# Feed-forward up projection of a decoder trunk: the second block of each loaded pair by seven half-size products in place of eight

## The chip, the cores and the metric

One core of one Trainium2 chip. The metric is the time of one execution on the device in microseconds (us), from which a median is taken over several runs. Times inside the profile are of one profiled execution of the same kernel.

## The reference, cut to what matters

```python
def _swiglu(h, w_up, w_down):
    u, gte = _split(h @ w_up, [D_FF, D_FF])
    return (jax.nn.silu(u) * gte) @ w_down
...
# each of DEPTH = 2 layers, every sub-layer wrapped as
#   x <- LN(alpha * x + gate * sublayer(modulate(x)))
#   feed-forward, token mixer (three branches and an out projection), feed-forward
```

The sizes are D_MODEL = 1024, SEQ = 512 tokens, D_FF = 2816, all float32. There are four feed-forwards (called FFN0 to FFN3 here, two per layer). Each computes 2816 columns of u and 2816 columns of g from 1024 inputs for 512 tokens, multiplies silu(u) by g, and projects back to 1024.

## The kernel before, in words

**Products.** A float32 product is made of three matmuls. Every operand is split into `hi` (rounded to the matmul's type) and `lo` (what is left), and `mm3` (L199 to L203) adds hi by hi, one cross term and the other cross term into the same PSUM bank. The activations stand in SBUF as `hhi` and `hlo`, 8 blocks of 128 inputs by 512 tokens. Weights come by DMA (SP's queue) into a ring of three `raw` tiles of 2048 floats and are split by `split_w` (L186): ACT copies `hi` (L194), and DVE subtracts `lo` (L196), or POOL where `on_pool` is set. That is so for chunk 0 of FFN1 to FFN3 and in the mixers.

**Slots.** The split weights live in slots that rotate (`slot`, L156): four in the pool `weights` ("base") and five more in a pool that is opened per stage ("ext", `WEXT`). A mode, base, ext or all, says which of them the next split takes. A split has to wait until the matmuls that read the slot's last content are done.

**One feed-forward** (`ffn`, L452). The 2816 columns are 22 blocks of 128, and they are worked in five chunks of 4, 4, 4, 5 and 5 blocks. In a chunk, each block is two products, u and g, of 8 input blocks by three matmuls of 512 tokens (24 and 24 matmuls of 128x512). Each has its own PSUM bank, from a rotation of four. Then ACT takes silu (L479), DVE multiplies (L480), and the result is split into `ahi` and `alo` (ACT L649, DVE L650). After the chunk's blocks, its down projection adds 128x512 products into eight banks, those of the rotation among them (`token_major`, `accumulators`). Chunks 0 to 3 are then evicted to the residual by DVE (`evict`, L553 and L554); the last chunk runs the norms of the next stage (`finish`, L410, `modulate`). In chunks 1 to 4 the blocks are loaded in pairs, one raw tile of u and one of g for two blocks. Chunk 0 is made while the previous stage's norms end: its first three blocks run in halves of 256 tokens, and block 3 as a whole. Between the blocks `bg_step` runs pieces of a vector by matrix product on DVE (L282, L284) for later stages.

**Order.** A scheduler writes each engine's list ahead of time. At run time every engine works through its list in order and waits by semaphores.

The changed code touches `ffn` (the chunk's loop over pairs), `ada` in its form for the start of the program, the mixer's out projection, and the size of the ext pool.

Of the kernel before, what the change touches and what calls it, by code (L numbers as in the profile page):

```python
# [9 lines left out]
F32 = mybir.dt.float32  # L10
# [21 lines left out]
WBASE = {"raw": 3, "hi": 4}  # L32
WEXT = {"raw": 0, "hi": 5}
BANKS = {"g": 2, "s": 3, "r": 2, "c": 1}
# [25 lines left out]
class Trunk:  # L60
    def __init__(self, ctx, tc, a, out):
# [3 lines left out]
        self.n = 0  # L65
        self.on_pool = False
        self.wmode, self.wcount = "all", {"raw": -1, "hi": -1}
# [182 lines left out]
    def ada(self, l, v, q, dst, mul=1.0):  # L250
# [6 lines left out]
        if self.starting:  # L257

            ps = self.ps("c")
            for kk in range(0, KB, 4):  # L260
                rs = [self.we.tile([P, 2, 512], F32, tag=tag, bufs=WEXT["hi"], name=self.nm("ada")) for tag in ("hi", "lo")]
                for i, r in enumerate(rs):
# [171 lines left out]


    def token_major(self, acc, lhs, rhs, first, last, kbs, by_tile, then=None, halves=False):

# [20 lines left out]
    def ffn(self, l, f, sub, nxt, begin):  # L458
# [3 lines left out]
        with self.tc.tile_pool(name=self.nm("ffn"), bufs=1, reuse_waits="tile") as fp:  # L462
# [10 lines left out]
            def up_mm(pss, ws, *part):  # L473
                for ps, w in zip(pss, ws):
                    self.gemm_part(ps, w, *part)

            def up_act(pss, hi, lo):
# [10 lines left out]
            for c, n in enumerate(CHUNKS):  # L488
# [26 lines left out]
                while j < n:  # L515
                    m = min(2, n - j)
                    for i, r in enumerate(up_load(b0 + j, m)):
                        pss = [self.ps("g"), self.ps("g")]
                        with later(c):
                            ws = [self.split_w(w) for w in r]  # L520
                        up_mm(pss, ws, 0, S)
                        up_act(pss, ahi[:, j + i, :], alo[:, j + i, :])
# [802 lines left out]
    def mixer(self, l, nxt):  # L1325
# [175 lines left out]
```

## Time and profile before

| | |
|---|---|
| median of 3 runs | 3094.02 us (3092.88 to 3103.51) |
| the profiled execution | 3098.59 us |
| its span (first to last instruction) | 3096.5 us |
| mean granted TensorE clock | 0.983 |
| PE busy | 2931.2 us, 95% of the span |
| DVE busy | 1880.0 us, 61% |
| ACT busy | 1142.2 us, 37% |
| POOL busy | 554.8 us, 18% |

The four feed-forwards lie at about 0 to 370 us, 1183 to 1555, 1555 to 1925 and 2725 to 3096; the mixers lie between. PE is TensorE's matmuls, PEld its loading of weights. A timeline row gives the start, the duration, the engine, the line, the operation, the output and inputs, and in brackets the idle time before it with what ended it. A matmul's duration runs from its start to its modelled end and overlaps the next one's, so the pace is read from start to start.

### The profile page before, as it was taken

To read this page: it belongs to the slowest core of one execution; us is meant where nothing else is said; L and a number is where in the kernel's file an instruction comes from. 1 tells how busy PE (TensorE), PEld (TensorE's weight loads), DVE (VectorE), ACT (ScalarE), POOL (GpSimd) and SP (SyncE) were. 2 spreads that over 40 slices of the span, in tenths; PEclk is the share of its full clock that TensorE was granted. 3 is DMA by queue.
4 is the path that set the end of the run, shared out by engine and by line. 5 is a ranking of instruction groups with operands and counts; after the bars stand their busy time and mean duration, and the time that the engine had idled before them with its cause. 6 is when DMAs were issued, how large, how long until landed. Compare 5 with 4: busy or idle time off the path is not lost. (4 is left out here: it accounts for less than half of the span.)

```text
span 3096.5 us, 39351 instructions
## 1 busy us (share of the span) xinstructions
PE 2931.2 (95%) x15330; PEld 2338.4 (76%) x15330; DVE 1880.0 (61%) x3534; ACT 1142.2 (37%) x1699; POOL 554.8 (18%) x379
## 2 busy tenths in 40 slices
PE   7999998998989998999999999889989899999998
PEld 5888886676766788888888887767666677788887
DVE  6755567666785656565656546667676756654435
ACT  4322253332545635222342214433335554342212
POOL 0000142333232013000130002423333320230000
PEclk9999999999999999999999999999999999999999
DMA  8634333333342463434434424433333424632221
GB/s 280 224 109 146 115 117 101 88 87 102 94 113 67 139 203 118 139 122 143 129 117 136 133 92 145 127 99 93 88 90 93 107 73 143 204 116 96 89 68 62
DMA packets 389402, 372.17 MB, mean 120 GB/s; under 512 B 54964, under 2 KB 318544, under 8 KB 389216
## 3 DMA queue, kind: packets, MB, share of 16 engines
q1 hardware_dynamic: 377048, 350.14, 37.0%
q10 hardware_dynamic: 12168, 19.53, 1.7%
q8 instruction: 120, 1.97, 0.3%
q14 instruction: 66, 0.54, 0.1%
HBM read 347.54 MB, written 22.09 MB: 119 GB/s over the span
## 5 line engine op out<-in xcount | busy, mean ns | idle before, releaser
L194 ACT ACTIVATE hi<-raw 128x1024 fp32r<-128x1024 f32 (+1 forms) x460 | 469.2, 1028 | 1248.9 <-PE pg L202 501.3
L196 POOL TENSOR_TENSOR lo<-raw,hi 128x1024 fp32r<-128x1024 f32 x164 | 408.0, 2490 | 1692.1 <-ACT hi L194 1639.2
L201 PE MATMUL pg<-hhi,hi 128*128 128x512 f32 (+1 forms) x1744 | 680.4, 393 | 13.7 <-DVE ks L645 3.7
L202 PE MATMUL pg<-hlo,hi 128*128 128x512 f32 (+1 forms) x1744 | 673.5, 389 | 2.9 <-DVE nm L343 2.9
L203 PE MATMUL pg<-hhi,lo 128*128 128x512 f32 (+1 forms) x1744 | 674.8, 391 | 0.0
L196 DVE TENSOR_TENSOR lo<-raw,hi 128x1024 fp32r<-128x1024 f32 (+1 forms) x296 | 342.5, 1165 | 301.3 <-ACT hi L194 296.1
L201 PEld LDWEIGHTS pg<-hhi,hi 128*128 128x128 f32 x1744 | 330.9, 190 | 86.9 <-issue 10.5
L203 PEld LDWEIGHTS pg<-hhi,lo 128*128 128x128 f32 x1744 | 330.6, 190 | 66.5 <-issue 2.1
L202 PEld LDWEIGHTS pg<-hlo,hi 128*128 128x128 f32 x1744 | 331.2, 190 | 65.3 <-issue 4.7
L202 PE MATMUL pr<-hlo,hi 128*128 128x512 f32 (+1 forms) x816 | 300.4, 368 | 5.1 <-DVE nm L343 2.9
L201 PE MATMUL pr<-hhi,hi 128*128 128x512 f32 (+1 forms) x816 | 301.5, 370 | 2.2 <-ACT hhi L397 2.2
L203 PE MATMUL pr<-hhi,lo 128*128 128x512 f32 (+1 forms) x816 | 300.7, 369 | 0.0
L284 DVE SCALAR_TENSOR_TENSOR acc<-raw,cact,acc 128x512 f32<-128x512 f32 x224 | 187.7, 838 | 48.7 <-DMA raw<-in_ada_w_dram 44.3
L202 PEld LDWEIGHTS pr<-hlo,hi 128*128 128x128 f32 x816 | 155.0, 190 | 34.2 <-issue 7.4
L201 PEld LDWEIGHTS pr<-hhi,hi 128*128 128x128 f32 x816 | 155.1, 190 | 28.1 <-ACT hhi L397 2.6
L203 PEld LDWEIGHTS pr<-hhi,lo 128*128 128x128 f32 x816 | 155.2, 190 | 27.4
L352 POOL TENSOR_TENSOR rstd<-var,mhalf 128x1 f32<-128x1 f32 x48 | 30.2, 630 | 470.5 <-DVE var L351 461.9
L201 PE MATMUL ps<-hi,ahi 128*128 128x512 f32 x264 | 103.5, 392 | 0.0
L203 PE MATMUL ps<-hi,alo 128*128 128x512 f32 x264 | 103.3, 391 | 0.0
L202 PE MATMUL ps<-lo,ahi 128*128 128x512 f32 x264 | 103.1, 391 | 0.0
L480 DVE TENSOR_TENSOR su<-pg,su 128x512 f32<-128x512 f32 x42 | 28.9, 689 | 115.2 <-PE pg L203 115.1
L480 DVE TENSOR_TENSOR su<-pr,su 128x512 f32<-128x512 f32 x42 | 29.0, 690 | 110.0 <-PE pr L203 105.9
(443 smaller groups left out, 4956.9 us busy)
## 6 DMA issues: line engine op xcount, KB each, us to landing
raw<-in_ffn_up_dram SPq DMA_DIRECT2D x70, 1024.0 KB
raw<-in_w_in_dram SPq DMA_DIRECT2D x132, 512.0 KB
raw<-in_ada_w_dram SPq DMA_DIRECT2D x64, 1024.0 KB
raw<-in_ffn_down_dram SPq DMA_DIRECT2D x40, 1024.0 KB
raw<-in_ffn_up_dram SPq DMA_DIRECT2D x36, 512.0 KB
gspill<-gate ACTq DMA_DIRECT2D x48, 256.0 KB
gate<-gspill SPq DMA_DIRECT2D x48, 256.0 KB
ada<-in_ada_w_dram SPq DMA_DIRECT2D x16, 512.0 KB
```

The lines of the kernel that those rows point to most:

```text
L194: self.nc.scalar.activation(hi, v, AF.Copy)
L196: eng.tensor_tensor(out=lo, in0=v, in1=hi.bitcast(F32), op=ALU.subtract)
L201: mm(out=ps, lhsT=lhi, rhs=rhi, start=start, stop=False, **kw)
L202: mm(out=ps, lhsT=lhi, rhs=rlo, start=False, stop=False, **kw)
L203: return mm(out=ps, lhsT=llo, rhs=rhi, start=False, stop=stop, **kw).ins
L284: nc.vector.scalar_tensor_tensor(out=acc, in0=r[:, i, :], scalar=c, in1=acc, op0=ALU.mult, op1=ALU.add)
L352: nc.gpsimd.tensor_tensor(out=r, in0=v, in1=self.mhalf, op=ALU.pow)
L480: nc.vector.tensor_tensor(out=su, in0=pss[1], in1=su, op=ALU.mult)
```

## The change

In chunks 1 to 4 the second block of every pair is no longer computed by two products of 8 input blocks by 512 tokens. The pair (u, g) of that block is seen as a 2 by 2 arrangement of weights (u and g, by input blocks 0 to 3 and 4 to 7), and the activations as 2 by 2 (input blocks 0 to 3 and 4 to 7, by tokens 0 to 255 and 256 to 511). Eight products of a quarter each would make that; the changed code makes it of seven (Strassen's scheme in Winograd's form). So 84 matmuls of 128x256 stand for 48 of 128x512. It is done for 8 blocks of each feed-forward, 32 in all.

- `combine` makes four sums of activation quarters once per feed-forward, in front of chunk 0's down projection: four operations of 128x1024 on DVE, four on POOL, then four splits (ACT L460, DVE L461) into eight new `T` tiles. It borrows `lng`, `lnb` and `gb` as scratch, so the load of `gb` for the feed-forward (L317) comes after it.
- `weight_sums` makes four sums of weight quarters per pair, all on POOL (128x512 each, L471 to L474). `seven_weights` splits u's weights, the two tiles of sums and half of g's. That last half has one buffer of its own (`g2hi`, `g2lo`).
- `seven` runs the seven products into three banks x, y and z. Running sums are carried in the banks, with copies by ACT between products (L503, L507, L509, L511), adds by DVE (L505, L514) and POOL (L512), one silu (L515), and two multiplications (L517, L518).
- To make room for T, the ext pool has 2 slots instead of 5. The program's first loads, the mixer's out projection and the last chunk's down projection take their slots accordingly.

```diff
-WEXT = {"raw": 0, "hi": 5}
+WEXT = {"raw": 0, "hi": 2}
...
+    def combine(self):
+        a, b, d = (t.rearrange("p (k s) -> p k s", k=4) for t in (self.lng, self.lnb, self.gb))
...
+        v(out=a, in0=hi[1], in1=lo[1], op=ALU.add)
+        g(out=b, in0=hi[3], in1=lo[3], op=ALU.add)
+        v(out=c, in0=a, in1=hi[0], op=ALU.subtract)
+        v(out=c, in0=c, in1=lo[0], op=ALU.subtract)
+        g(out=d, in0=b, in1=a, op=ALU.subtract)
+        v(out=a, in0=b, in1=c, op=ALU.subtract)
+        g(out=b, in0=hi[2], in1=a, op=ALU.subtract)
+        g(out=b, in0=b, in1=lo[2], op=ALU.add)
+        for i, t in enumerate((a, c, d, b)):
+            nc.scalar.activation(self.T[i][0], t, AF.Copy)
+            v(out=self.T[i][1], in0=t, in1=self.T[i][0].bitcast(F32), op=ALU.subtract)
...
+    def seven_weights(self, u, g, a, b):
+        for v in (u, a, b):
+            hi, lo = self.split_w(v)
+            ws += [(hi[:, k], lo[:, k]) for k in (k1, k2)]
+        hi, lo = (self.we.tile([P, 4, P], F32R, tag=n, name=self.nm(n)) for n in ("g2hi", "g2lo"))
+        self.split_act(g[:, k2], hi, lo)
+        return ws + [(hi, lo)]
...
+        product(0, x, True)
+        act(s1, x, AF.Copy)
+        product(1, y, True)
+        v(out=s1, in0=s1, in1=y, op=ALU.add)
+        product(2, x, False)
+        act(s2, x, AF.Copy)
+        product(3, z, True)
+        act(p5, z, AF.Copy)
+        product(4, x, False)
+        act(u3, x, AF.Copy)
+        nc.gpsimd.tensor_tensor(out=u3, in0=u3, in1=p5, op=ALU.add)
+        product(5, z, False)
+        v(out=s2, in0=s2, in1=z, op=ALU.add)
+        act(su, su, AF.Silu)
+        product(6, x, False)
+        v(out=s1, in0=s1, in1=x, op=ALU.mult)
+        v(out=s2, in0=s2, in1=u3, op=ALU.mult)
...
+                    rs = up_load(b0 + j, m)
+                    if c and m == 2:
+                        sums = self.weight_sums(*rs[1])
+                    for i, r in enumerate(rs):
+                        if c and i:
+                            up_pair(r, sums, ahi[:, j + i, :], alo[:, j + i, :])
...
                 if c == 0:
+                    self.combine()
...
-                ws += [self.split_w(r[:, i : i + 1, :], *((xp, 1) if k + i == KB - 1 else ())) for i in range(2)]
+                if k == 6:
+                    self.wmode = "base"
...
+                ws += [self.split_w(r[:, i : i + 1, :], *((xp, 2) if k == 4 else ())) for i in range(2)]
```

Three places of the order are shown. In the changed program L194 and L196 are still `split_w`, L747 is `split_act`, L570 the silu of an ordinary block.

ACT's list during a block of seven products, in chunk 1 of FFN0 (`su_1119` is that block's sum, `hc` holds P5 and U3, `s` are the sums of weights):

```order
L194 ACTIVATE hi_1303<-raw_1226 128x1024
L747 ACTIVATE ahi_1018<-su_1088 128x512
L503 ACTIVATE su_1119<-pg_1120 128x256
L194 ACTIVATE hi_1307<-s_1230 128x1024
L507 ACTIVATE su_1119<-pg_1120 128x256
L194 ACTIVATE hi_1311<-s_1231 128x1024
L509 ACTIVATE hc_1123<-pr_1122 128x256
L511 ACTIVATE hc_1123<-pg_1120 128x256
L194 ACTIVATE hi_1439<-raw_1437 128x1024
L515 ACTIVATE su_1119<-su_1119 128x512
L747 ACTIVATE g2hi_1315<-raw_1228 128x512
L747 ACTIVATE ahi_1018<-su_1119 128x512
```

Three splits for a later block now stand among the copies out of PSUM, one in front of the copies L507 and L509 each. All 32 blocks have this order.

POOL's list at the start of FFN1, before (raw_10124 and raw_10114 are chunk 0's down weights, raw_10039 holds block 3's u and g):

```order
L196 TENSOR_TENSOR lo_10127<-raw_10124,hi_10126 128x1024
L196 TENSOR_TENSOR lo_10131<-raw_10124,hi_10130 128x1024
L196 TENSOR_TENSOR lo_10045<-raw_10039,hi_10044 128x1024
L196 TENSOR_TENSOR lo_10049<-raw_10039,hi_10048 128x1024
L196 TENSOR_TENSOR lo_10117<-raw_10114,hi_10116 128x1024
L196 TENSOR_TENSOR lo_10121<-raw_10114,hi_10120 128x1024
```

and now (block 3's weights are raw_10544, u first and g second; the down weights are raw_10644 and raw_10654):

```order
L452 TENSOR_TENSOR lnb_9746<-hhi,hlo 128x1024
L455 TENSOR_TENSOR gb_9744<-lnb_9746,lng_9745 128x1024
L457 TENSOR_TENSOR lnb_9746<-hhi,lng_9745 128x1024
L458 TENSOR_TENSOR lnb_9746<-lnb_9746,hlo 128x1024
L196 TENSOR_TENSOR lo_10550<-raw_10544,hi_10549 128x1024
L196 TENSOR_TENSOR lo_10651<-raw_10644,hi_10650 128x1024
L196 TENSOR_TENSOR lo_10657<-raw_10654,hi_10656 128x1024
L196 TENSOR_TENSOR lo_10661<-raw_10654,hi_10660 128x1024
L196 TENSOR_TENSOR lo_10554<-raw_10544,hi_10553 128x1024
L196 TENSOR_TENSOR lo_10647<-raw_10644,hi_10646 128x1024
L471 TENSOR_TENSOR s_10786<-raw_10784 128x512
```

The four operations of `combine` stand ahead of all of them, and the `lo` of block 3's g has moved from fourth of six to ninth of ten, behind three of the down weights.

ACT's list a little later in the same stage, now (`su_10605` is block 3, raw_10782 and raw_10784 are the first pair of chunk 1):

```order
L570 ACTIVATE su_10539<-pc_10327 128x512
L194 ACTIVATE hi_10646<-raw_10644 128x1024
L747 ACTIVATE ahi_10202<-su_10539 128x512
L747 ACTIVATE g2hi_10877<-raw_10784 128x512
L194 ACTIVATE hi_10794<-raw_10782 128x1024
L570 ACTIVATE su_10605<-pg_10547 128x512
```

The half split of g for chunk 1's first pair stands in front of block 3's silu. Its raw tile is loaded by SP behind the reload of `gb`, and takes the place in the ring of a down tile of which POOL's `lo_10647` is the last reader. Before, the four splits of the first pair (u and g of both its blocks) stood ahead of block 3's silu.

## Rows read from the trace of the kernel before

**Rows 1.** The page, part 1: busy time and share of each engine.

```profile
PE 2931.2 (95%) x15330; PEld 2338.4 (76%) x15330; DVE 1880.0 (61%) x3534; ACT 1142.2 (37%) x1699; POOL 554.8 (18%) x379
```

**Rows 2.** Waits of PE, 1206 to 1550 us (FFN1): us in total, times, longest.

```profile
PE pg L201 <- DVE su L480: 0.6, 1, 0.6
PE pc L374 <- ACT xn L368: 0.4, 1, 0.4
```

**Rows 3.** The same, 1540 to 1620 us (from FFN1 into FFN2).

```profile
PE pr L202 <- DVE var L351: 2.2, 1, 2.2
PE pr L201 <- ACT hhi L397: 2.2, 1, 2.2
```

**Rows 4.** Timeline of PE: four blocks, from their first matmul to the down projection's first.

```profile
1256.48 0.39 PE L201 MATMUL pr<-hhi,hi 128*128 128x512 f32 x1
...
1301.28 0.39 PE L201 MATMUL pr<-hi,ahi 128*128 128x512 f32 x1
```

**Rows 5.** Timeline of PE: matmuls of 128x256, two stretches of chunk 0 of FFN1.

```profile
1193.42 0.28 PE L201 MATMUL pr<-hhi,hi 128*128 128x256 f32 x1
...
1197.66 0.28 PE L201 MATMUL pr<-hhi,hi 128*128 128x256 f32 x1
...
1206.28 0.28 PE L201 MATMUL pg<-hhi,hi 128*128 128x256 f32 x1
...
1210.02 0.28 PE L201 MATMUL pg<-hhi,hi 128*128 128x256 f32 x1
```

**Rows 6.** Groups by line and shape, weight loads: busy us, mean ns, idle before.

```profile
L202 PEld LDWEIGHTS pg<-hlo,hi 128*128 128x128 f32 x1744 | 331.2, 190 | 65.3 <-issue 4.7
```

**Rows 7.** Groups by line and shape, ACT.

```profile
L194 ACT ACTIVATE hi<-raw 128x1024 fp32r<-128x1024 f32 x428 | 449.2, 1058 | 1195.9 <-PE pg L202 475.8 <-PE pr L202 325.7 <-PE ps L203 156.8
L649 ACT ACTIVATE whi<-wf 128x256 fp32r<-128x256 f32 x16 | 6.4, 401 | 0.0
```

**Rows 8.** Groups by line and shape, DVE and POOL.

```profile
L196 DVE TENSOR_TENSOR lo<-raw,hi 128x1024 fp32r<-128x1024 f32 x264 | 320.5, 1223 | 300.1 <-ACT hi L194 294.9
...
L196 DVE TENSOR_TENSOR lo<-raw,hi 128x512 fp32r<-128x512 f32 x32 | 21.9, 686 | 1.2 <-ACT hi L194 1.2
...
L196 POOL TENSOR_TENSOR lo<-raw,hi 128x1024 fp32r<-128x1024 f32 x164 | 408.0, 2490 | 1692.1 <-ACT hi L194 1639.2 <-PE pg L203 16.9 <-DMA wf<-in_rwkv_w_dram 12.9
...
L1275 POOL TENSOR_TENSOR bout<-i,ge 128x512 f32<-128x512 f32 x16 | 21.8, 1365 | 137.6 <-DVE i L1274 123.5 <-ACT Y L894 14.1
```

**Rows 9.** Timelines of POOL and DVE at the start of FFN1.

```profile
1181.88 2.62 POOL L196 TENSOR_TENSOR lo<-raw,hi 128x1024 fp32r<-128x1024 f32 x1 [0.95 <-ACT hi L194]
...
1215.38 8.12 POOL L196 TENSOR_TENSOR lo<-raw,hi 128x1024 fp32r<-128x1024 f32 x3 [2.75 <-ACT hi L194]
...
1182.18 3.40 DVE L399 TENSOR_TENSOR hlo<-hf,hhi 128x1024 fp32r<-128x1024 f32 x1
...
1216.91 1.52 DVE L650 TENSOR_TENSOR alo<-su,ahi 128x512 fp32r<-128x512 f32 x1 [0.70 <-ACT ahi L649]
```

**Rows 10.** Windows of FFN1 (stretch; busy us of PE, PEld, DVE, ACT, POOL; PEclk; DMA).

```profile
1206.00:1234.50 28.50, 28.50 (x200) 26.37 (x200) 14.54 (x17) 13.16 (x16) 12.63 (x5) 1.00 0.52 165
...
1256.40:1301.20 44.80, 44.80 (x194) 36.18 (x193) 23.18 (x29) 12.23 (x15) 0.00 (x0) 1.00 0.48 153
1301.20:1323.00 21.80, 21.80 (x98) 18.02 (x97) 13.00 (x19) 4.85 (x5) 0.00 (x0) 1.00 0.20 72
```

**Rows 11.** Windows at the start of FFN2, the same columns.

```profile
1561.00:1564.00 3.00, 0.62 (x3) 0.41 (x3) 3.00 (x4) 1.33 (x3) 1.84 (x1) 0.89 0.04 3
1564.00:1567.00 3.00, 2.93 (x14) 2.96 (x15) 2.46 (x8) 1.32 (x2) 0.86 (x1) 0.50 0.88 328
```

**Rows 12.** Timelines of SP, ACT, DVE and PE, chunk 0 of FFN1.

```profile
1208.16 10.12 SPq L182 DMA_DIRECT2D raw<-in_ffn_up_dram  x2
...
1213.29 2.01 ACT L194 ACTIVATE hi<-raw 128x1024 fp32r<-128x1024 f32 x2 [1.24 <-DMA raw<-in_ffn_up_dram]
...
1202.28 1.22 DVE L399 TENSOR_TENSOR hlo<-hf,hhi 128x1024 fp32r<-128x1024 f32 x1 [1.19 <-ACT hhi L397]
...
1222.60 0.39 PE L201 MATMUL pg<-hhi,hi 128*128 128x512 f32 x1
...
1233.59 0.39 PE L201 MATMUL pr<-hi,ahi 128*128 128x512 f32 x1
```

More of the change, by code (lines that the diff above doesn't have):

```diff
@@ L65, in __init__ @@
         self.n = 0
-        self.on_pool = False
+        self.on_pool, self.etile = False, -1
         self.wmode, self.wcount = "all", {"raw": -1, "hi": -1}
@@ L260, in ada @@
             for kk in range(0, KB, 4):
-                rs = [self.we.tile([P, 2, 512], F32, tag=tag, bufs=WEXT["hi"], name=self.nm("ada")) for tag in ("hi", "lo")]
+                rs = []
+                for _ in range(2):
+                    i = self.etile = (self.etile + 1) % 12
+                    tag, bufs = (("T", 8), ("hi", WEXT["hi"]), ("T", 8), ("T", 8), ("lo", WEXT["hi"]), ("T", 8))[i % 6]
+                    rs.append(self.we.tile([P, 2, 512], F32, tag=tag, bufs=bufs, name=self.nm("ada")))
                 for i, r in enumerate(rs):
@@ new lines, in weight_sums @@
+    def weight_sums(self, u, g):
+        nc = self.nc
+        a, b = (self.lp.tile([P, D], F32, tag="xn", bufs=2, name=self.nm("s")).rearrange("p (k c) -> p k c", k=KB) for _ in range(2))
+        t = nc.gpsimd.tensor_tensor
+        k1, k2 = slice(0, 4), slice(4, 8)
+        t(out=a[:, k2], in0=g[:, k1], in1=g[:, k2], op=ALU.add)
+        t(out=a[:, k1], in0=a[:, k2], in1=u[:, k1], op=ALU.subtract)
+        t(out=b[:, k1], in0=u[:, k1], in1=g[:, k1], op=ALU.subtract)
+        t(out=b[:, k2], in0=u[:, k2], in1=a[:, k1], op=ALU.subtract)
+        return a, b
@@ new lines, in seven_weights, with seven, product @@
+    def seven_weights(self, u, g, a, b):
+        k1, k2 = slice(0, 4), slice(4, 8)
+        ws = []
+        for v in (u, a, b):
[4 more added lines that the diff above has]
+        return ws + [(hi, lo)]
+    def seven(self, ws, su):
+        nc = self.nc
+        act, v = nc.scalar.activation, nc.vector.tensor_tensor
+        x, y, z = (self.ps("g")[:, 0:256] for _ in range(3))
+        c = self.lp.tile([P, KB, P], F32, tag="hf", bufs=1, name=self.nm("hc")).rearrange("p k s -> p (k s)")
+        p5, u3 = c[:, 0:256], c[:, 256:512]
+        s1, s2 = su[:, 0:256], su[:, 256:S]
+        def product(i, out, start):
+            (whi, wlo), (rhi, rlo) = ws[i], self.h7[i]
+            for k in range(4):
+                self.mm3(out, whi[:, k, :], wlo[:, k, :], rhi[:, k, :], rlo[:, k, :], start and k == 0, k == 3, skip_group_check=True)
+        product(0, x, True)
[15 more added lines that the diff above has]
+        v(out=s2, in0=s2, in1=u3, op=ALU.mult)
@@ L475, in up_mm, with up_pair @@
                     self.gemm_part(ps, w, *part)
+            def up_pair(r, sums, hi, lo):
+                ws = self.seven_weights(*r, *sums)
+                su = fp.tile([P, S], F32, tag="su", bufs=2, name=self.nm("su"))
+                self.seven(ws, su)
+                self.split_act(su, hi, lo)
             def up_act(pss, hi, lo):
@@ L516, in ffn @@
                     m = min(2, n - j)
[L517 to L522, printed above, removed]
+                    rs = up_load(b0 + j, m)
[4 more added lines that the diff above has]
+                            up_pair(r, sums, ahi[:, j + i, :], alo[:, j + i, :])
+                        else:
+                            pss = [self.ps("g"), self.ps("g")]
+                            with later(c):
+                                ws = [self.split_w(w) for w in r]
+                            up_mm(pss, ws, 0, S)
+                            up_act(pss, ahi[:, j + i, :], alo[:, j + i, :])
                         if c:
```

8 lines of the change are left out of this document (added).

## The prediction, made before the changed kernel was run

> **What bounds the kernel now.** I read the page's totals first, to see which engine there is to save on: PE is busy for 95% of the span, DVE for 61%, POOL for 18% [rows 1]. Whether a cut in PE's work is a cut in time then depends on whether PE waits, so the second view is PE's waits in a feed-forward. From 1206 to 1550 us, chunks 0 to 4 of FFN1, it waited 1.0 us in all [rows 2]. The reader is to see there that the feed-forward is bound by the issue of matmuls alone. Only where one stage passes into the next does PE stand, for example 2.2 and 2.2 us into FFN2, on the norm's chain of DVE and ACT operations [rows 3]. So every microsecond of matmul taken out counts in full, unless a wait appears that has no row yet. The third view, the timelines, is where I looked for such waits: what an engine would need to be late by.
>
> **What it removes.** Four ordinary blocks, 192 matmuls of 128x512, run from 1256.48 to 1301.28, 44.80 us, 0.2333 us each [rows 4]. A block is 48 of them, 11.20 us. It becomes 84 of 128x256. Their pace has two rows: 36 in 4.24 us (0.1178) and 33 in 3.74 us (0.1133) [rows 5]. I take half of the 512's own pace, 0.1167, because both shapes stand at the same granted clock of 1.00 [rows 10] and it lies between the two. Then the seven cost 9.80 us and a block gains 1.40; 32 blocks gain **44.8 us**. With 0.1133 it would be 53.8, with 0.1178 41.7: the bounds. A weight load shows 190 ns of busy time [rows 6], more than a 256's pace, but the 256s of rows 5 each came with their own load, so loads overlap and I give them no price.
>
> The trace's steps of 0.2333 and 0.1133 to 0.1178 can be set against a rule. The Trainium skill, "TensorE: Matmul & The Clock Gate", section "Back-to-back issue gap", gives N/2.4 + 2.5 ns for an isolated matmul at the full clock, a fixed part that half-size matmuls pay twice as often. By it a block would gain 1.19 us and the sum of gains would be 38 us; the rows show no such fixed part clearly, since one of the two stretches is faster than half.
>
> **What it adds on the way of PE, in each seven-block.** Three places.
> - *The copy of P5.* Product 5 adds onto bank z, so PE must wait until ACT has copied P5 out. Cover: product 4, 12 matmuls, 1.40 us. In ACT's list a weight split stands in front of that copy, and the slot it fills is the one that product 3 was the last to read, so it cannot go earlier. From product 3's end: 1.06 for the split and 0.40 for a copy of 128x256 [rows 7], 1.46 with a few hundredths for each handover. I take 0.15 late, 32 times, **5 us**; 0 if the split finds its slot free, 0.5 each (16) if it is later still.
> - *Bank x at the chunk's down projection.* The last multiplication reads x after product 7; the down projection needs all eight banks. In chunks 1 and 2, where the chunk ends with a seven-block, 8 times, about 0.4 each: **3 us** (0 to 8). Chunks 3 and 4 end with an ordinary block.
> - *Weights.* The second block now needs three and a half splits instead of two, in six slots instead of nine, and two of them wait for POOL's sums: four operations of 128x512 at about 1.37 (the nearest row of that shape), 5.5 us per pair, then two splits. The pair's loads run a block ahead, 11.2 us; I cost it at nothing. If that cover goes, each of the 32 pairs could wait a microsecond or two; that is rival C.
>
> **What it adds once per feed-forward: combine.** It stands in front of block 3 on POOL, which does the `lo` of chunk 0. DVE and POOL hinder each other here: a DVE subtraction of 128x1024 that takes 1.22 alone [rows 12] took 3.40 when a POOL subtraction of 2.62 had begun 0.3 before it, and an `alo` took 1.52 during POOL's three [rows 9], against 0.69 for the same shape from weights [rows 8]. So I add the two engines up as if one held the other off. The last `hlo` ends at 1203.5 [rows 12]. From there POOL has four sums and five `lo` up to that of block 3's g, 9 at 2.4 to 2.5, 22 us [rows 8], and DVE's four sums and four subtractions, 8 at 1.22, 9.8 us, of which about 8 us fall between POOL's, with the `alo`. That is some 31 us, so it ends near 1235. PE needs it where block 3's second product starts, 24 matmuls after 1222.60 [rows 12], that is at 1228. **PE is about 6 us late** in FFN1. Then block 3's silu stands behind the half split of the first pair's g. That tile's place in the ring is freed by POOL's last `lo`, and a transfer took 5.1 us from issue to ACT's start [rows 12]. Chunk 0's down projection begins with its first two blocks meanwhile (48 matmuls, some 11 us at the step of rows 4), so most of this is covered; I take 3 us. Together **9 us** each in FFN1 and FFN3, whose lists agree, and 4 in FFN2, where POOL does block 3 earlier: **22 us** (0, if DVE slips between without delay, to 35). In FFN0, chunk 0 lies in the start of the program, and DVE is busy enough that eight more operations cost perhaps **3 us** (0 to 8).
>
> **The clock.** After idle gaps of 2.2 us, matmuls at FFN2's start ran at a granted clock of 0.50 for some 5 us, 0.213 apart instead of 0.117 [rows 11]. Each new gap of 6 us may be followed by as much: 3 to 5 us of stretch at half speed loses 1.5 to 2.5. **4 us** in all (0 to 8).
>
> **Boundaries.** With two ext slots, the last chunk's down weights take three of four base slots and hold them to the end. The next stage's first splits then start late; they stood in the shadow of the norm chain [rows 3]. I take 1.5 us at each of four, **6 us** (0 to 12).
>
> **Sum.** -44.8 + 5 + 3 + 22 + 3 + 4 + 6 = -1.8 us on the profiled execution's 3098.6 (span 3096.5 and 2.1 around it), 3096.8. The median of the runs shown stands 4.6 us below the profiled one, so the forecast is **3092 us**. A measurement of this kernel can tell about 0.5%, 15.5 us, from no change.
>
> **The rivals.**
> - *A, the forecast (0.40).* The stalls return most of the gain; the net lies within 15 us. For it: the order of POOL's and ACT's lists at three feed-forwards. Against it: each of six terms is a bound from a distant row.
> - *B, the covers hold (0.36).* DVE and POOL interleave better than rows 9 say, P5 is never late, boundaries don't move. Costs of 12 us, the floor of the terms that have a row (P5 5, combine 7): -44.8 + 12 = -33, so **3061 us**. For it: in chunk 0's window DVE is busy for only 14.5 of 28.5 us and POOL for 12.6 [rows 10].
> - *C, DVE and POOL together become the bound of the chunks (0.22), slower.* In a four-block chunk DVE works 23.2 + 13.0 us of 66.6 [rows 10] and POOL nothing. The change adds per pair two adds, three more half-size operations and 5.5 us or more of POOL, about 6 us of DVE and 12 of POOL per chunk. If POOL and DVE exclude each other as in rows 9, that makes 54 of the 63.8 us left. Lists are in order, so waits would appear at weights and at the adds between products. At 1.5 us in each of 16 chunks it gives +24 on the forecast, **3116 us**; it decides from about 1 us per chunk. The Trainium skill, "SBUF — State Buffer", section "SBUF: two separate sides", says that the pair of ports which DVE and GpSimd share is locked for a whole instruction, for DVE with two SBUF inputs too; the 3.40 beside 2.62 agrees, and by it POOL's four sums would hold up every `lo` behind them.
> - *D, half-size matmuls bound by their weight load (0.02).* 84 at 0.19 make 16 us, +4.8 per block, +154: about 3245. The paces of rows 5 speak against it.
> - That the change doesn't do what it says is excluded: PE's list grows by 1152 instructions, 32 times 36.
>
> **How the numbers follow.** A, the likeliest, has a range of its own of 3077 to 3107, B one of 3050 to 3075, C one of 3105 to 3135. The range of 3055 to 3118 leaves out the best of B, the worst of C, and D. Faster by over 0.5% is B and little of A: 0.38; within it most of A and the near edge of C: 0.39; slower 0.23.
>
> **What would show it.** PE's step in a seven-block at 0.117, and a block's 84 in 9.8 us. PE's wait for ACT's L509 32 times at 0.1 to 0.2. At the start of FFN1 and FFN3 a wait of PE for POOL's `lo` of 5 us or more, and a granted clock under 1 behind it. In the chunks POOL's L471 to L474 at 1.4 each, with DVE's L196 stretched beside them but no wait of PE on DVE. The forecast is wrong if PE's waits in FFN1 sum to under 4 us (then B), or if PE waits in chunks 1 to 4 for `lo` or for DVE's L505 and L514 by a microsecond and more each (then C).

## The result, and the profile after

The changed kernel takes **3146.7 us** (median of 4, 3144.1 to 3148.1) against 3094.6 for the kernel before: a ratio of **1.016, 95% interval 1.014 to 1.018**. It is slower by 52 us, where 3092 was forecast and 3118 was the end of the range. The sign is that of rival C, beyond the 3135 us that C reached, and the mechanism is for the most part not C's.

The page's first part, the same line as [rows 1]:

```profile
PE 2930.5 (93%) x16482; PEld 2381.7 (76%) x16482; DVE 2137.6 (68%) x3726; ACT 1253.3 (40%) x1907; POOL 858.5 (27%) x555
```

PE is as busy as before, 2930.5 against 2931.2 us, with 1152 matmul instructions more. DVE works 258 us more, POOL 304, ACT 111. So the saving on PE, if there is one, is eaten on PE itself or hidden in slower stretches, and the page can't say which.

What says it is a table of stretches. From PE's timeline I took the start of the first matmul of each piece of the four feed-forwards, in both traces: the first half-block of chunk 0, each chunk's first down matmul, and the first matmul of chunk 1. Each row is a length in the kernel after minus that in the kernel before, in us:

```
                                            FFN0    FFN1    FFN2    FFN3
first half-block to chunk 0's down*         +4.6   +10.3    +5.3    +9.1
chunk 0's down projection                   +5.0    +7.3   +10.6    +1.5
chunks 1 to 4, up to the last down          -4.8    -6.6    -0.8    -6.5
passage and mixer ahead of it**                 -    +8.1    +0.1    +2.4
*  FFN0: from the start of the span
** FFN3: and the end of the span
```

The four starts lose 53.7 us, chunks 1 to 4 gain 18.7, and the rest loses 10.7: 45.6 us between the two profiled executions (spans 3142.2 and 3096.5). In the kernel before, FFN0's last down projection begins only at 379.1 us, so FFN0 reaches past the 370 us that were given for it.

**The sevens.** PE's timeline of one block of seven products, chunk 2 of FFN0: its first matmul, the place at which product 5 waits for P5, and the next block's first matmul.

```profile
194.12 0.28 PE L201 MATMUL pr<-hhi,hi 128*128 128x256 f32 x1
...
201.01 0.28 PE L203 MATMUL pr<-T,lo 128*128 128x256 f32 x1
201.25 0.38 PE L201 MATMUL pg<-hhi,hi 128*128 128x256 f32 x1
201.47 0.28 PE L202 MATMUL pg<-hlo,hi 128*128 128x256 f32 x1
...
204.14 0.40 PE L201 MATMUL pg<-hhi,hi 128*128 128x512 f32 x1
```

The block takes 10.02 us. Steps are 0.24 and 0.22 at product 5 instead of 0.12: that is P5, and it costs some 0.2, where 0.15 was forecast. The median of all 32 is 10.1 us, against 11.1 for the mean ordinary block. Four of five run like that. Seven take longer, 10.3 to 14.0, 9 us in all.

**The start of FFN1**, the waits of PE from 1196 to 1290 us, without two for the norms (1.2 and 0.2); before, from 1206 us on, the longest wait in chunk 0 was 0.6 us [rows 2]:

```profile
PE pg L201 <- DVE su L571: 6.2, 1, 6.2
PE pg L201 <- ACT hi L194: 3.2, 1, 3.2
PE pg L202 <- DVE nm L347: 2.2, 1, 2.2
PE pg L203 <- POOL lo L196: 2.0, 1, 2.0
```

Two waits of 3.2 and 2.0 us for block 3's second weight, then one of 6.2 for a bank. The first two make 5.2 us, where the prediction asked for 5 or more on POOL's `lo`; only 2.0 of them are for `lo`, the 3.2 are for ACT's `hi`. They come from here, the timelines of POOL, DVE and ACT:

```profile
1218.39 3.44 POOL L452 TENSOR_TENSOR lnb<-hhi,hlo 128x1024 f32<-128x1024 f32 x1 [6.62 <-DVE hlo L403]
1221.91 3.26 POOL L455 TENSOR_TENSOR gb<-lnb,lng 128x1024 f32<-128x1024 f32 x1
...
1233.40 18.41 POOL L196 TENSOR_TENSOR lo<-raw,hi 128x1024 fp32r<-128x1024 f32 x6
...
1218.34 1.23 DVE L451 TENSOR_TENSOR lng<-hhi,hlo 128x1024 f32<-128x1024 f32 x1
1219.61 3.31 DVE L453 TENSOR_TENSOR hc<-lng,hhi 128x1024 f32<-128x1024 f32 x1
1222.95 3.31 DVE L454 TENSOR_TENSOR hc<-hc,hlo 128x1024 f32<-128x1024 f32 x1
1226.36 1.23 DVE L456 TENSOR_TENSOR lng<-lnb,hc 128x1024 f32<-128x1024 f32 x1
...
1240.61 3.43 DVE L461 TENSOR_TENSOR T<-lnb,T 128x1024 fp32r<-128x1024 f32 x1
1243.96 0.68 DVE L571 TENSOR_TENSOR su<-pr,su 128x512 f32<-128x512 f32 x1
...
1244.67 0.63 ACT L747 ACTIVATE ahi<-su 128x512 fp32r<-128x512 f32 x1 [6.44 <-DVE su L571]
1245.21 1.04 ACT L194 ACTIVATE hi<-raw 128x1024 fp32r<-128x1024 f32 x1
```

DVE's sums take 1.23 alone and 3.31 while POOL works; POOL's take 3.3 beside DVE. POOL's six subtractions run 3.07 each instead of 2.4 to 2.5 [rows 8], because DVE has its own subtractions of combine at the same time, and the last ends at 1251.8. ACT's split of block 3's second weight, at 1245.21, stands behind a split that waited 6.44 us for a multiplication on DVE, and DVE was busy with combine. POOL comes to its own subtraction for that weight at the same time, 1246.33.

The wait of 6.2 us, in PE's timeline of the down projection, now and (last row) before:

```profile
1258.66 0.39 PE L203 MATMUL pg<-hi,alo 128*128 128x512 f32 x1
1265.23 0.80 PE L201 MATMUL pg<-hi,ahi 128*128 128x512 f32 x1 [6.18 <-DVE su L571]
...
1236.39 0.50 PE L201 MATMUL pg<-hi,ahi 128*128 128x512 f32 x1 [0.55 <-DVE su L480]
```

The down projection had begun at 1256.83. It adds the first block's products into its eight banks in turn, three matmuls each, so PE comes to the fourth bank with its tenth matmul, after some 2 us. That bank still holds block 3's product, and PE waits until block 3's multiplication (L571) has read it. Before, the wait of 0.6 us in [rows 2] stood in front of the same tenth matmul.

Why that multiplication is late: the tile of g for the next pair is loaded when POOL's fifth subtraction ends, at 1249.02 (not the sixth, `lo_10647`, which ends at 1251.81). From there the chain goes on on SP, ACT and DVE:

```profile
1249.05 0.37 SPq L182 DMA_DIRECT2D raw<-in_ffn_up_dram  x1
...
1255.80 0.63 ACT L747 ACTIVATE g2hi<-raw 128x512 fp32r<-128x512 f32 x1 [7.60 <-DMA raw<-in_ffn_up_dram]
...
1257.28 0.58 ACT L570 ACTIVATE su<-pg 128x512 f32<-128x512 f32 x1
...
1258.80 2.25 POOL L472 TENSOR_TENSOR s<-s,raw 128x512 f32<-128x512 f32 x1
...
1259.85 1.48 DVE L286 TENSOR_SCALAR acc<-raw,cact 128x512 f32<-128x512 f32 x1
1261.37 3.21 DVE L288 SCALAR_TENSOR_TENSOR acc<-raw,cact,acc 128x512 f32<-128x512 f32 x3
1264.49 0.68 DVE L571 TENSOR_TENSOR su<-pg,su 128x512 f32<-128x512 f32 x1
```

ACT stands 7.6 us idle in front of the half split `g2hi`, with block 3's silu behind it. When silu is done, at 1257.9, its multiplication still stands on DVE behind a split and four pieces of the vector product (L286, L288), which POOL's weight sums stretch (1.48 where the same line took 0.48 before). It starts at 1264.49. That is the wait of 6.2.

In FFN2 the silu and the multiplication of block 3 hold a bank each, and PE stands in front of its seventh and its tenth matmul (the vector product also waits 1.24 us there for its weights):

```profile
1646.08 0.50 PE L201 MATMUL pr<-hi,ahi 128*128 128x512 f32 x1 [1.60 <-ACT su L570]
...
1653.90 0.80 PE L201 MATMUL pr<-hi,ahi 128*128 128x512 f32 x1 [6.86 <-DVE su L571]
```

The clock follows, in the windows of the same stretch (columns as in [rows 10]):

```profile
1250.00:1257.00 7.00, 7.00 (x22) 5.50 (x21) 0.54 (x1) 1.21 (x2) 2.97 (x2) 0.67 0.98 334
1257.00:1261.00 4.00, 2.05 (x9) 1.33 (x8) 4.00 (x3) 1.81 (x3) 4.00 (x3) 1.00 0.01 6
1261.00:1267.00 6.00, 1.77 (x4) 1.50 (x5) 5.80 (x7) 0.64 (x1) 1.37 (x2) 0.54 0.21 52
1267.00:1272.00 5.00, 5.00 (x20) 4.00 (x20) 2.21 (x4) 1.06 (x1) 0.00 (x0) 0.87 0.97 341
```

The granted clock is 0.67 for 7 us after the first two waits, with the two levels mixed in that window (PE's matmuls are 0.43 us apart up to 1254.4 and 0.23 after), and 0.54 during the third, where PE hardly works. In 1250 to 1257 PE is busy all the time and issues 22 matmuls where 30 would fit at 0.2333: an estimate of 1.9 us lost in that stretch alone.

**The slow sevens.** In four of the seven, PE waits 0.6 to 1.2 us for the copy out of bank x (L503). Here the one of FFN2's last chunk, timelines of POOL, DVE, ACT and PE:

```profile
1899.53 1.30 POOL L473 TENSOR_TENSOR s<-raw,raw 128x512 f32<-128x512 f32 x1
...
1899.59 1.52 DVE L286 TENSOR_SCALAR acc<-raw,cact 128x512 f32<-128x512 f32 x1 [1.18 <-DMA raw<-in_ada_w_dram]
1901.14 2.46 DVE L288 SCALAR_TENSOR_TENSOR acc<-raw,cact,acc 128x512 f32<-128x512 f32 x2
1903.52 0.69 DVE L571 TENSOR_TENSOR su<-pg,su 128x512 f32<-128x512 f32 x1
...
1904.24 0.63 ACT L747 ACTIVATE ahi<-su 128x512 fp32r<-128x512 f32 x1 [1.65 <-DVE su L571]
1904.78 0.36 ACT L503 ACTIVATE su<-pr 128x256 f32<-128x256 f32 x1
...
1905.20 0.39 PE L201 MATMUL pr<-T,hi 128*128 128x256 f32 x1 [0.65 <-ACT su L503]
```

POOL's weight sum holds the vector product up, DVE's multiplication of the block before is late, ACT's split of it too, and the copy out of bank x stands behind that split. The four share this end; what makes DVE late differs. In chunk 4 of FFN0 (340.5 us) it is again the vector product beside two of POOL's sums. In the last slow block of FFN2 (1924 us) POOL does nothing, and the product itself waits 0.83 us for a transfer. In the first block of FFN0 DVE is busy with evictions and splits, at their usual length. So rival C's mechanism, DVE and POOL holding each other up, is seen at two of 32 blocks, at about 1 us each, not at 1.5 us in each of 16 chunks. (The longest of the seven, 14.0 us in FFN2, is another: PE waits 2.1 us there for a transfer of the mixer's vectors.)

### The profile page after: what moved, and what is told of

The parts are those of the page before. It is cut to its first block, busy times and chain, and to the rows that moved or that the text cites. A ratio compares the mean times of both kernels' runs of the same rounds, so it can differ in the third digit from the quotient of the medians.

```text
span 3142.2 us, 42455 instructions
## 1 busy us (share of the span) xinstructions
PE 2930.5 (93%) x16482; PEld 2381.7 (76%) x16482; DVE 2137.6 (68%) x3726; ACT 1253.3 (40%) x1907; POOL 858.5 (27%) x555
## 5 line engine op out<-in xcount | busy, mean ns | idle before, releaser
L194 ACT ACTIVATE hi<-raw 128x1024 fp32r<-128x1024 f32 (+1 forms) x428 | 436.7, 1025 | 811.5 <-PE pg L202 340.0
L201 PE MATMUL pg<-hhi,hi 128*128 128x512 f32 (+1 forms) x1680 | 638.0, 383 | 17.0 <-DVE ks L743 3.5
L202 PE MATMUL pg<-hlo,hi 128*128 128x512 f32 (+1 forms) x1680 | 631.9, 379 | 4.3 <-DVE nm L347 2.2
L196 POOL TENSOR_TENSOR lo<-raw,hi 128x1024 fp32r<-128x1024 f32 x164 | 420.1, 2566 | 782.2 <-ACT hi L194 741.2
L203 PE MATMUL pg<-hhi,lo 128*128 128x512 f32 (+1 forms) x1680 | 631.2, 379 | 2.0 <-POOL lo L196 2.0
L196 DVE TENSOR_TENSOR lo<-raw,hi 128x1024 fp32r<-128x1024 f32 (+1 forms) x264 | 331.7, 1261 | 176.8 <-ACT hi L194 174.8
L201 PE MATMUL pr<-hhi,hi 128*128 128x256 f32 (+1 forms) x752 | 256.5, 342 | 7.0 <-ACT hi L194 3.2
L202 PE MATMUL pr<-hlo,hi 128*128 128x256 f32 (+1 forms) x752 | 255.3, 340 | 6.7 <-DVE var L355 2.3
L203 PE MATMUL pr<-hhi,lo 128*128 128x256 f32 (+1 forms) x752 | 254.4, 338 | 1.6 <-POOL lo L196 1.6
L288 DVE SCALAR_TENSOR_TENSOR acc<-raw,cact,acc 128x512 f32<-128x512 f32 x224 | 194.3, 868 | 32.2 <-DMA raw<-in_ada_w_dram 28.5
L471 POOL TENSOR_TENSOR s<-raw 128x512 f32<-128x512 f32 x32 | 43.6, 1363 | 448.3 <-DVE lo L196 220.0
L194 ACT ACTIVATE hi<-s 128x1024 fp32r<-128x1024 f32 x64 | 67.9, 1060 | 240.0 <-PE ps L203 137.3
L196 DVE TENSOR_TENSOR lo<-s,hi 128x1024 fp32r<-128x1024 f32 x64 | 78.2, 1222 | 76.9 <-ACT hi L194 76.7
L512 POOL TENSOR_TENSOR hc<-hc 128x256 f32<-128x256 f32 x32 | 29.0, 906 | 325.4 <-ACT hc L511 325.4
```

The lines of the kernel that those rows point to most:

```text
L194: self.nc.scalar.activation(hi, v, AF.Copy)
L196: eng.tensor_tensor(out=lo, in0=v, in1=hi.bitcast(F32), op=ALU.subtract)
L201: mm(out=ps, lhsT=lhi, rhs=rhi, start=start, stop=False, **kw)
L202: mm(out=ps, lhsT=lhi, rhs=rlo, start=False, stop=False, **kw)
L203: return mm(out=ps, lhsT=llo, rhs=rhi, start=False, stop=stop, **kw).ins
L288: nc.vector.scalar_tensor_tensor(out=acc, in0=r[:, i, :], scalar=c, in1=acc, op0=ALU.mult, op1=ALU.add)
```

## The experiments

Before is 3092 to 3095 us on the chips of these runs. "Starts", "chunks" and "rest" are the sums of the table's rows over the four feed-forwards, against the kernel before (the change: +53.7, -18.7, +10.7).

**1. Combine without its sums.**

```diff
-        v(out=a, in0=hi[1], in1=lo[1], op=ALU.add)
...
-        g(out=b, in0=b, in1=lo[2], op=ALU.add)
-        for i, t in enumerate((a, c, d, b)):
+        for i, t in enumerate((hi[1], hi[0], hi[2], hi[3])):
```

> Leaves out the eight sums of combine (four on DVE, four on POOL); the T tiles are still made, of the plain quarters of the activations, so the sevens' results are not the sums they should be. Theory: the loss of the changed kernel sits at the four starts (chunk 0 of each feed-forward takes 9.1, 17.5, 15.9 and 10.6 us longer in its trace, 53 in all), because combine's sums hold POOL and DVE up, and everything behind them is late. Then at least 35 of the 53 us go and the time is about 3105 to 3112 us. Rival one, the order: what delays block 3 is the split of g's half for the next pair in front of its silu, with the ring and the transfer behind it, with or without the sums. Then under 15 us go, about 3130 to 3147. Rival two, the sevens and the smaller pool cost it elsewhere: no change, 3147.

Measured: 3106.5 us, ratio 1.005 (1.0035 to 1.0059). Starts +13.3, chunks -14.3, rest +4.7. Of the 53.7 us at the starts 40 go. The theory holds: eight operations of 1.2 to 2.4 us, once per feed-forward, make most of the loss. The kernel is still not faster than before.

**2. Combine alone, no sevens.**

```diff
-                    if c and m == 2:
-                        sums = self.weight_sums(*rs[1])
...
-                        if c and i:
-                            up_pair(r, sums, ahi[:, j + i, :], alo[:, j + i, :])
-                        else:
+                        if True:
```

> The second blocks are computed as before (48 matmuls of 128x512), with no sums of weights and no half split; combine stays with all its operations, and so do the smaller pool and the other moved slots. Theory: combine alone makes block 3's weights late at three starts, some 5 us of wait and 2 to 4 us of half clock each, and boundaries cost some 10: before + 25 to 35, 3120 to 3130 us, with the 26 us of the sevens missing from the gain and the wait behind the half split missing from the cost. Rival, the half split's order is the whole cost: chunk 0 as before within 2 us each, about 3095 to 3108.

Measured: 3153.4 us, ratio 1.019 (1.017 to 1.021). Starts +45.6, chunks +0.1, rest +8.4. Against both numbers: the starts lose nearly what they lose in the full change, though there is no half split. Its trace has the waits of 3.2 and 1.6 for block 3's weight, and 3.0 in front of the tenth matmul of the down projection in FFN1:

```profile
PE pg L201 <- ACT hi L194: 3.2, 1, 3.2
PE pg L201 <- DVE su L571: 3.0, 1, 3.0
PE pg L203 <- POOL lo L196: 1.6, 1, 1.6
```

The first pair's ordinary splits stand in front of block 3's silu just as the half split does. I had taken the second wait for a matter of the half split alone.

**3. Block 3's silu first.**

```diff
+    def behind(self):
+        es = ExitStack()
+        for ins in getattr(self, "hold", None) or ():
+            es.enter_context(self.tc.issue_after(ins))
+        return es
...
-                ws = self.seven_weights(*r, *sums)
+                with self.behind():
+                    ws = self.seven_weights(*r, *sums)
...
+                    self.hold = self.last_ahi, self.last_alo
                     self.combine()
```

> The changed kernel, with chunk 1's first pair (its splits, the half split, and the pieces of the vector product between) ordered behind block 3's last split on ACT and DVE. Theory: block 3's silu no longer waits for the next pair's transfer; the wait of 6.2 us of PE for DVE's L571 in FFN1, 6.9 in FFN2 and 1.0 in FFN3, and some of the half clock after them, go: 12 to 20 us, about 3127 to 3135. The 3.2 + 2.0 us of wait for block 3's weights stay. Rival, POOL alone is late and the order only passes it on: under 4 us, 3143 to 3147.

Measured: 3124.0 us, ratio 1.0095 (1.0075 to 1.0115), 23 us under the change, 3 more than the theory allowed. Starts +35.3, chunks -17.3, rest +7.7. In FFN1 the wait for L571 is gone and the other two stand, to a tenth:

```profile
PE pg L201 <- ACT hi L194: 3.2, 1, 3.2
PE pg L202 <- DVE nm L347: 2.2, 1, 2.2
PE pg L203 <- POOL lo L196: 2.0, 1, 2.0
```

So the starts' loss has two parts that can be taken apart: combine's lateness on POOL, and the order in which the next pair passes that lateness on to block 3. The order is worth 18 us, and it is the whole loss of the down projections in FFN1 and FFN2 (+7.3 and +10.6 in the change, -0.6 and 0.0 here).

**4. Combine on DVE, in its place.**

```diff
-        v, g = nc.vector.tensor_tensor, nc.gpsimd.tensor_tensor
+        v = g = nc.vector.tensor_tensor
```

> The changed kernel with all eight sums of combine on DVE, none on POOL, in the same place. Theory: the price of combine is that DVE's and POOL's operations stretch one another (DVE's sums took 3.31 instead of 1.23, POOL's 3.3 instead of 2.4, and five of six of POOL's subtractions 3.07 on the mean), so that POOL's subtractions start some 15 us late. With POOL free of it, the three late starts lose at least half of their excess (FFN1 17.5, FFN2 15.9, FFN3 10.6): 3118 to 3130 us. Rival, the number of operations: DVE's eight more hold up the splits of blocks 0 to 2 as long as POOL's did those of block 3, no gain: 3140 to 3150.

Measured: 3134.1 us, ratio 1.013 (1.010 to 1.016). Starts +37.6, chunks -14.2, rest +14.3. The three late starts (FFN1 to FFN3) fall from 44.0 to 33.8, a quarter and not half, so neither number holds. In FFN1 the stretch up to the down projection loses 3.9 instead of 10.3, and the down projection 9.9 instead of 7.3: what POOL no longer delays, the wait for the bank of block 3's product (6.3) takes up again. Experiment 8 puts the two edits together.

**5. Combine late, 24 sevens.**

```diff
-        a, b, d = (t.rearrange("p (k s) -> p k s", k=4) for t in (self.lng, self.lnb, self.gb))
+        x = self.lp.tile([P, D], F32, tag="xn", bufs=2, name=self.nm("d"))
+        a, b, d = (t.rearrange("p (k s) -> p k s", k=4) for t in (self.lng, self.lnb, x))
...
+        v = g = nc.vector.tensor_tensor
...
-                        if c and i:
+                        if c >= 2 and i:
...
+                    if c == 1 and j == 2:
+                        with self.tc.issue_after(self.last_ahi), self.tc.issue_after(self.last_alo):
+                            self.combine()
```

> Combine is moved to the middle of chunk 1 (behind its first pair), all its operations on DVE, its fourth scratch another tile, so that the gate vector is not held; the sevens begin with chunk 2, 24 blocks instead of 32. Theory: the starts come back to what they were before the change (within 2 us each), the sevens give 24 x 1.1 = 26 us, the boundaries and mixers keep some 10: about 3080 us, faster than both. Rival, the load of DVE and POOL in the chunks: the waits move to chunks 1 and 2, PE waits for weights there by several us in each feed-forward, about 3100 to 3115.

Measured: 3103.1 us, ratio 1.0028 (1.0017 to 1.0039). Starts +8.8, chunks -10.4, rest +5.6. The starts come back but for FFN2's, +5.8. The forecast of 3080 was missed all the same: 24 sevens gave 10 us and not 26, and what was left at the boundaries took it back. The number is the rival's, but PE waits for no weights in the chunks.

Where the sevens' gain goes can be read against the kernel of experiment 6, which has the same pool and no sevens. There the blocks of chunks 1 to 4 take 798.3 us, here 782.1: 16 us and not 26, since the median of the 24 is 10.1 us and six of them are slow by 6 us together. And the down projections take 293.9 us instead of 288.3. Most of that is chunk 1's, 0.9 to 1.3 us longer in each feed-forward: PE waits 0.7 to 1.0 us there for a multiplication (L572), which DVE reaches late behind combine. What the boundaries are is the next question.

**6. Only the pool.**

```diff
-                    if c and m == 2:
-                        sums = self.weight_sums(*rs[1])
...
-                        if c and i:
-                            up_pair(r, sums, ahi[:, j + i, :], alo[:, j + i, :])
-                        else:
+                        if True:
...
-                    self.combine()
```

> Of the change only the smaller ext pool and the moved slots stay (the program's first loads, the out projection, the last chunk's down weights); no combine, no sevens, no sums of weights. Theory: what is left in every variant so far, 5.5 us at FFN2's start and some us between FFN0 and FFN1, comes from the last chunk's down weights, which now hold three of four base slots and push the next stage's splits into the norm chain: +8 to +15 us, 3102 to 3109, with +5 to 6 at FFN2's start and the chunks within 0.5 us each. Rival, it belongs to the eight T tiles or to the sevens: same as before within 4 us, 3090 to 3098.

Measured: 3116.7 us, ratio 1.007 (1.004 to 1.010). Starts +9.6, of which FFN2 +5.7; chunks +0.2; rest +9.9, of which +10.4 between FFN0's last down projection and FFN1. More than expected: the smaller pool by itself costs some 20 us. FFN2's start shows the way, in ACT's, POOL's and DVE's timelines:

```profile
1574.41 2.00 ACT L194 ACTIVATE hi<-raw 128x1024 fp32r<-128x1024 f32 x2
...
1577.17 5.15 POOL L196 TENSOR_TENSOR lo<-raw,hi 128x1024 fp32r<-128x1024 f32 x2
...
1580.57 2.83 DVE L425 SCALAR_TENSOR_TENSOR tmp<-xt,mean,lng 128x1024 f32<-128x1024 f32 x1
...
1585.47 3.42 DVE L433 SCALAR_TENSOR_TENSOR xt<-tmp,rstd,lnb 128x1024 f32<-128x1024 f32 x1 [0.73 <-POOL rstd L356]
```

The two splits had to wait for base slots that the last down weights held. Now their subtractions on POOL fall among the norm's operations on DVE, which take 2.83 and 3.42 where they took 1.28 and 1.29, and PE waits 4.4 us for the norm (L372) where it had waited 0.7.

**7. The last down weights in T tiles.** They are free by then. To the late combine:

```diff
+                            if last and j + i >= WEXT["hi"]:
+                                hi, lo = (self.we.tile([P, 1, D], F32R, tag="T", bufs=8, name=self.nm("dw")) for _ in range(2))
+                                self.split_act(r[:, i : i + 1, :], hi, lo)
+                                ws.append((hi, lo))
+                            else:
+                                ws.append(self.split_w(r[:, i : i + 1, :]))
```

> The kernel with the late combine (24 sevens from chunk 2 on), and the last chunk's third to fifth down weights in T tiles, which are free by then, instead of base slots. Theory: FFN2's start comes back by 5 us and the passage from FFN0 to FFN1 by 2 to 5: 3090 to 3096 us, still no clear gain on before, since the sevens' 26 us shrink to 10 in the chunks. Rival, the boundary's loss is the order of the norms and not the slots: as e4, 3099 to 3107.

Measured: **3085.9 us, ratio 0.9975 (0.9964 to 0.9987)**. Starts +3.4, chunks -12.6, rest -3.4. This version beats both kernels, by 9 us or a quarter of a percent against the kernel before, with the first stretch of FFN2 back to -0.4. The theory had it at 3090 to 3096; 4.4 us of the profile's gain lie in the mixer ahead of FFN3, which is not explained (experiment 9).

The same edit to the kernel with only the smaller pool:

> Only the smaller pool with the last down weights in T tiles; no combine, no sevens. It is the kernel with the late combine and the T tiles without its 24 sevens. Theory: the boundaries stand as before the change and the chunks' down projections keep the 2 to 3 us that the pool alone cost them: 3094 to 3100 us, so that the 24 sevens with their combine are worth 8 to 14 us. Rival, moving the slots is itself a gain and the sevens bring nothing: 3084 to 3089.

Measured: 3095.9 us, ratio 1.0013 (1.0004 to 1.0023). As the theory had it. Starts +2.8, chunks +0.0, rest -2.0: against experiment 6 the edit takes 7 us from the starts and 12 from the rest. The passages can be followed up to the mixer's first matmul of 128x32, which comes 72 to 75 us after the last chunk's first down matmul in the kernel before. Up to there experiment 6 loses 5.5 us behind FFN0 and 2.1 behind FFN2 (the change itself 7.1 and 3.3), and this kernel -0.5 and +0.4. All seven kernels with the last down weights in base slots lose 5.5 to 7.1 and 2.1 to 5.0 us there, and 5.3 to 6.1 in FFN2's first stretch; the four with T tiles lose -1.1 to +0.4 at all three. So the held base slots cost some 13 of experiment 6's 20 us, and the edit takes all of it back. The other 4 us of the 12 lie further on in the mixers. And 24 sevens with their combine are worth 0.38% by the two ratios, 12 us, and 13.5 by the profiles (12.7 in the chunks).

**8. All 32 sevens, with what was learned.** Experiments 3 and 4 together, and the T tiles.

> All 32 sevens, combine in its first place but wholly on DVE, chunk 1's first pair ordered behind block 3's split, and the last chunk's down weights in T tiles. Theory: the starts keep 2 to 4 us of excess each, the boundaries none, the chunks give 19 to 22: 3080 to 3090 us, faster than before. Rival, DVE's longer list at the start delays the first down projection as combine on POOL did: 3100 to 3115.

Measured: 3094.0 us, ratio 0.9999 (0.9987 to 1.0010). Between theory and rival. Starts +11.0, chunks -10.1, rest -4.0. The edits that took 18, 16 and (the T tiles) 7 us from the starts singly take 43 together: at the starts they add up. But the first seven-block of FFN0 and FFN1 now takes 16.9 us instead of 10.1. PE waits 4.2 and 4.6 us there for the copy out of bank x, behind a multiplication that DVE reaches late. The splits of that pair were moved behind block 3, but so they were in experiment 3, whose longest block, beside one of 14.3, takes 11.5; why they cost this much here is not shown. The loss moved once more.

**9. 28 sevens.** The version of 7 with combine behind block 3's split and the sevens from chunk 1's second pair:

```diff
-                        if c >= 2 and i:
+                        if (c, j) >= (1, 2) and i:
```

> As the kernel with the late combine and T tiles for the last down weights, but combine (on DVE) stands right behind block 3's split, beside chunk 0's down projection, and the sevens begin with chunk 1's second pair: 28 instead of 24. Theory: four more sevens at 1.1 each, nothing lost at the starts: 4 us under that kernel, some 0.4% under before, about 3080 to 3083 us. Rival, combine beside the evictions makes DVE late for chunk 1's weights: 3088 to 3096.

Measured: 3089.2 us, ratio 0.9994 (0.9984 to 1.0004). Starts +3.6, chunks -13.3, rest +4.5. The number lies in the rival's range, but in chunk 1 PE waits for DVE by no more than 0.4 us (L518). FFN0, FFN1 and FFN3 gain 4.9 to 6.1 us each in their chunks, 2 more than in 7. FFN2 loses 5.8 in chunk 1, where PE waits 4.3 us for a transfer of the mixer's vectors:

```profile
PE ps L687 <- DMA vrow<-in_rwkv_gn_b_dram: 4.3, 1, 4.3
```

The mixer ahead of FFN3 takes 5.4 us longer than before. The stretch with that mixer varied from -4.4 to +6.5 over these kernels, which all have the same mixer but for its slots, so differences of this size in "rest" are not read here.

## Why the prediction was wrong

The terms as the prediction put them, and as measured:

```
                                              predicted   measured
products and P5                                   -39.8      -21.5
bank x at the down projections                     +3.0       +2.7
combine, FFN0's start, the clock                  +29.0      +44.0
boundaries                                         +6.0      +20.5
sum                                                -1.8      +45.6
```

The measured first three lines are the lengths in the change's trace less those in the kernel with only the smaller pool (experiment 6): the blocks of chunks 1 to 4, their down projections, and the starts. The fourth is what that kernel loses by itself, 19.7 us, with the 0.8 by which the two differ in "rest". That the two parts add up is assumed.

- **The pace of the half-size matmuls: nearly right.** It is 0.118 to 0.119 in most products, against the 0.1167 taken; 0.1178 was the bound. With P5 the block takes 10.1 us, where 9.95 was the sum. That is 5 us over 32 blocks. That P5 is late, and why, was right; it is 0.2 us and not 0.15.
- **"I cost it at nothing" (the weights and what hangs on POOL's sums): wrong.** Seven slow blocks cost 9 us. POOL's four sums took 1.36 to 1.95 us on the mean, where 1.37 was taken. At two of the seven blocks the way is the one of rival C.
- **The gain per block was taken against 11.20; the mean ordinary block took 11.13 in the trace of before (801.2 us for 72), 11.09 with the smaller pool (798.3) and 11.11 in the change.** That is some 4 us more.
- **The down projections: right.** They lose 5.8 us, but 3.1 of these come with the smaller pool alone (experiment 6, 288.3 against 285.2 us for the 12 of chunks 1 to 3), where the blocks are 2.9 us shorter: a length that moved from one to the other. 2.7 us are left, of 3 forecast.
- **Combine, block 3's weights in FFN1 and FFN3: right.** PE waits 5.2 and 4.8 us for block 3's second weight, where 6 were forecast, with DVE and POOL stretching each other. 3.2 of each are a wait for ACT's split, which stands behind a multiplication that DVE reaches late; the prediction had POOL's list alone there.
- **Combine, the cover behind it: the step that failed.** "Chunk 0's down projection begins with its first two blocks meanwhile (48 matmuls, some 11 us at the step of rows 4), so most of this is covered; I take 3 us." PE got through 9 matmuls, some 2 us, and not 48: the tenth needs the bank that block 3's multiplication has still to read. It waited 6.2 us there in FFN1, and the wait was followed by more matmuls at half clock. The 0.6 us of [rows 2] showed, in the kernel before, that PE meets this bank. The multiplication is as late as it is since it stands behind pieces of the vector product, which POOL's weight sums then stretch.
- **"4 in FFN2, where POOL does block 3 earlier": the same step.** FFN2's start lost 15.9 us: 5.3 in its first stretch, where the smaller pool alone loses 5.7, and 10.6 in the down projection, with waits of 1.6 and 6.9 for banks of block 3. The order of POOL's list was read there and the order of ACT's and DVE's was not: the half split and the vector product stand in front of block 3's silu and multiplication in FFN2 as well, and experiment 3 takes those 10.6 us to zero. FFN0's 3 us were 9.6; PE stands 4.2 us there in front of the first down matmul, for ACT's split of its weight.
- **Boundaries, "1.5 us at each of four": mis-sized.** Three of them took 7.1 (FFN0 into the mixer), 5.3 (FFN1 into FFN2) and 3.3 us (FFN2 into the mixer). The mechanism was named, base slots held to the end, and it was priced as a late split "in the shadow of the norm chain". It is not in the shadow: the late split's subtraction on POOL runs into the norm's operations on DVE and makes the norm, which PE waits for, longer (shown at FFN2's start, experiment 6).
- **The sign.** Rival C had 0.22, slower by over 0.5% had 0.23, and its 3116 us were reached only by adding 24 to a forecast in which every cost was already low. Most of them were priced at one late operation, and the lateness had a second listener. That the time came out on C's side is luck for C: of the two signs that were to show the forecast wrong, neither came. PE's waits in FFN1 sum to 15 us and not to under 4, and in its chunks 1 to 4 the trace shows none.

The Trainium skill, "SBUF — State Buffer", section "SBUF: two separate sides", says of the pair of ports that DVE and GpSimd share that it is locked for a whole instruction. The trace agrees for operations with two SBUF inputs: DVE's 1.23 became 3.31 in step with POOL's 3.3.

What stays open: why the mixers' length moves by several us from one kernel to another, why the first seven-block is so late in experiment 8, and how much of the 53.7 us at the starts is the clock alone; no run here holds the clock.

## What to carry to other kernels

A change that saves on the engine that bounds the kernel and pays on the others has to be read at the passages, where those others end last: here 32 blocks gave 19 us in their chunks, and eight operations per feed-forward, in the one stretch where DVE and POOL are what PE waits for, took 40. For an operation that is made late, read on every engine's list what stands behind it, up to the next result or bank that the bounding engine needs; here the third wait was the largest. Where other work is to cover a wait, count how far that work comes before it needs something that the late operation still holds: here 9 matmuls of 48. And buffers that are taken away from a pool cost where they are held over a stage's end; giving the last users tiles that had become free returned 19 of 20 us in the profiles, some 14 of them at the three passages where the slots are held.

## What was not expected of the hardware

- DVE and POOL operations on SBUF hold each other off so evenly that both show nearly the sum of the two (3.6 us): DVE 3.31 (1.23 alone), POOL 3.26 and 3.44 (2.4 alone), two operations of each in a row.
- DVE's L286, one tensor by one scalar column, with a single large input, took 1.48 to 1.52 beside POOL's sums and 0.48 alone; DVE's L571, which reads PSUM, stayed at 0.68 or 0.69.
- A gap of 3.2 and 2.0 us in PE's work was followed by a window of 7 us at a granted clock of 0.67 in which PE had work all the time.
